# First norm of a transformer-like layer: gain and bias moved behind the transposes, and in token layout into the down stage

## The chip, the cores and the metric

One core of a Trainium2 chip runs the whole layer in one launch. The time is the device time of one execution in microseconds (us); the figure to compare is the median of several runs. Five engines work side by side: PE (matrix products), DVE (vector work), ACT (activations, copies and products with a scale), POOL (a slower vector engine) and SP, whose queue issues most of the transfers. Each works off its own instructions in the order in which the program was built, and stops where an instruction needs something that is not there yet.

## What is computed

One layer with 1024 tokens of width 1024: two mixing groups, an output projection, a residual and a layer norm, then a gated MLP of width 2816 with a causal convolution of width three on the gate branch, again a residual and a layer norm. The part that the change touches is the first norm and what reads its result:

```python
y = (xf - mu) * lax.rsqrt(var + LN_EPS) * g + b     # layer_norm
x = layer_norm(x * alpha + mix @ w_out, ln1_g, ln1_b)
h = causal_dwconv(x @ w_gate, conv_w, conv_b)
x = layer_norm(x * alpha + (silu(h) * (x @ w_up)) @ w_down, ln2_g, ln2_b)
```

So the normalised x is used twice: as the operand of the gate and up products, and as the residual behind the down product.

## The kernel before

Tokens lie in eight tiles t = 0 to 7 of 128 partitions. All large products are made in three matmuls each (`mm3`, L221 to L223) of 128x512, from operands that are split into a high part (ACT, L216) and a low part (DVE, L217).

**Output projection and first norm.** For each t PE makes the projection. `fill_x` adds the residual (DVE, L900) and takes the statistics (L901). `lnorm` then aggregates them (DVE, L882), adds epsilon (L884), raises to the power -1/2 (POOL, L885), and per half row subtracts the mean and multiplies by g (DVE, L887), scales (ACT, L889) and adds b (POOL, L890); for t = 7 DVE does the last step (L892). The rows g1 and b1, 128x1024 each, are loaded by POOL's queue (L873) ahead of that.

**Transposes.** `x1_transp(t)` transposes the eight 128x128 blocks of a tile (PE, L926), four to a PSUM bank, so that the width lies on partitions. ACT copies the blocks out (L934) and splits them; for A22 DVE adds A21 to the block straight out of PSUM (L931, the operand S1) and POOL forms A11 - A21 (L932). The tile's halves are called A11, A12 (tiles 0 to 3) and A21, A22 (tiles 4 to 7).

**Gate and up.** The stage uses Strassen-Winograd products: for each of 22 weight columns u seven products P1 to P7 of 12 matmuls each, instead of eight. Their left operands are A11, A12, A22 and the sums S1 = A21 + A22, S2 = S1 - A11, S3 = A11 - A21, S4 = A12 - S1. `x1_sums` makes S2 (DVE, L944) and S4 (POOL, L946) and splits all four; `w_prep` makes the sums of the weights (DVE, L968) and splits them. The first products need only A11 and A12, so tiles 6 and 7 and the sums are made between them (the list `fill_in`).

**Down stage.** The seven products run in the order P1, P2, P6, P5, P7, P4, P3, each over 11 steps m, from operands yo and do that `d_prepare` makes ahead; a pool of 20 slots holds them. Where a quarter of the output is done, DVE adds the residual x (L1223) and the second norm follows (`finish`). A pool of 16 larger slots (`kslot`) holds operands and rows.

The order on each engine is set where the program is built: it follows the order of the code and the slots that come free, not a table.

Of the kernel before, what the change touches and what calls it, by code (L numbers as in the profile page):

```python
# [138 lines left out]
def hybrid_layer_kernel(  # L139
# [90 lines left out]
    lam4 = const.tile([P, 4, 64], F32, name="lam4")  # L230
# [640 lines left out]
    def load_row(pool, ap_, name):  # L871
        t = pool.tile([P, D], F32, name=name)
        GP.dma_start(t, bc_row(ap_, D))  # L873
        return t

    g1 = load_row(op, ln1_g, "g1")
    b1 = load_row(op, ln1_b, "b1")
    x1T = {}
# [60 lines left out]
    def x1_sums(name):  # L939
        o = {"S1": "S1", "S2": "S1", "S3": "A21", "S4": "A12"}[name]  # L940
        x_operand(name, xslot if name in ("S1", "S2") else kslot)
# [314 lines left out]

    for n, name in enumerate(DORDER):
# [79 lines left out]
```

## Time and profile before

| | us |
|---|---|
| median of 3 runs | 1104.15 (1103.53 to 1104.35) |
| the profiled execution | 1102.54, its span 1100.8 |
| input projections | 0 to about 245 |
| attention | to about 375 |
| output projection, first norm, transposes | to about 455 |
| gate and up | 442 to 876 |
| down | 866 to 1092 |
| last norm and store | to 1100.8 |

The times of rows are counted from the span's start. A row of a timeline has the start, the length, the engine, the line, the operation, what it writes and reads, and how many instructions stand in it; a bracket at its end tells how long the engine was idle before it and what it waited for. Instructions that follow each other without a pause overlap a little, so the step from one to the next is shorter than the length shown: two of 1.21 in a row show 2.35 together.

### The profile page before, as it was taken

What the parts mean: (1) busy time and instruction counts of PE and PEld (TensorE: products, weight loads), DVE (VectorE), ACT (ScalarE), POOL (GpSimd) and SP (SyncE); (2) the same over time, 40 slices, a digit from 0 to 9 for tenths busy, and PEclk for the clock granted to TensorE, in tenths of its full rate; (3) what the DMA queues carried; (4) which work ended last, traced back from release to release, by engine and by line L of the source; (5) the groups of instructions that cost most, each with busy time, mean ns of one, the idle gap of its engine ahead of it and who ended that gap; (6) DMA issues with size and microseconds to landing.
All of it is one profiled execution on the core that took longest, in us unless ns stands there. A gap on an engine that the chain in (4) does not pass through costs nothing.

```text
span 1100.8 us, 13950 instructions
## 1 busy us (share of the span) xinstructions
PE 1063.5 (97%) x4974; PEld 873.8 (79%) x4974; DVE 806.4 (73%) x1331; ACT 488.1 (44%) x908; POOL 213.5 (19%) x233
## 2 busy tenths in 40 slices
PE   8999999889999999899999999999999999999995
PEld 6888887667788888678888888888888878888874
DVE  5327257789998648997787677778767679965786
ACT  5511113338777416564345344434534354444441
POOL 2014144466545126500000000000000000000045
PEclk9999999998999999999999999999999999999998
DMA  8400202111200421023323331332234883433322
GB/s 260 148 10 10 96 21 59 56 39 39 78 11 11 141 93 45 20 88 123 124 86 105 112 125 60 115 125 108 74 115 156 301 307 98 142 94 98 102 89 96
DMA packets 53222, 109.62 MB, mean 100 GB/s; under 512 B 6112, under 2 KB 6640, under 8 KB 53152
## 3 DMA queue, kind: packets, MB, share of 16 engines
q1 hardware_dynamic: 52112, 105.41, 28.4%
q0 software_dynamic: 1040, 3.32, 1.1%
q8 instruction: 39, 0.64, 0.3%
q14 instruction: 31, 0.25, 0.1%
HBM read 82.23 MB, written 24.38 MB: 97 GB/s over the span
## 4 chain that ended last, share of the span: by engine, by line
PE 78%; DVE 13%; POOL 2%; issue 2%; ACT 2%; DMA 1%; SPq 0%; DVEq 0%; POOLq 0%; ACTq 0%
PE ps L222 24%; PE ps L223 24%; PE ps L221 24%; DVE t L439 2%; PE ps L618 2%; POOL t L442 1%; DVE qs L471 1%; DVE p L587 1%; DVE x L887 1%; PE ps L604 1%; POOL uT L363 1%; PE ps L541 1%; DVE mx L554 1%; PE ps L542 1%; DMA xraw<-xT 1%
## 5 line engine op out<-in xcount | busy, mean ns | idle before, releaser
L222 PE MATMUL ps<-do,yo 128*128 128x512 f32 x308 | 120.9, 393 | 3.3 <-DVE do L217 3.3
L221 PE MATMUL ps<-do,yo 128*128 128x512 f32 x308 | 120.0, 391 | 2.5 <-ACT do L216 2.5
L223 PE MATMUL ps<-do,yo 128*128 128x512 f32 x308 | 120.3, 391 | 0.0
L1264 POOL DMA_DIRECT2D g<-ln_g x1 | 0.6, 578 | 476.0 <-DVE do L217 476.0
L217 DVE TENSOR_TENSOR wT<-wq,wT 128x512 fp32r<-128x512 f32 x88 | 63.1, 719 | 33.9 <-ACT wT L216 33.9
L216 ACT ACTIVATE wT<-wq 128x512 fp32r<-128x512 f32 x88 | 55.3, 632 | 50.2 <-PE ps L223 43.5
L217 DVE TENSOR_TENSOR yo<-ya,yo 128x512 fp32r<-128x512 f32 x77 | 55.0, 715 | 24.1 <-ACT yo L216 23.8
L222 PEld LDWEIGHTS ps<-do,yo 128*128 128x128 f32 x308 | 58.2, 189 | 16.8 <-DVE do L217 4.6
L221 PEld LDWEIGHTS ps<-do,yo 128*128 128x128 f32 x308 | 58.0, 189 | 15.2 <-ACT do L216 2.9
L216 ACT ACTIVATE yo<-ya 128x512 fp32r<-128x512 f32 x77 | 48.3, 627 | 48.1 <-PE ps L223 46.0
L223 PEld LDWEIGHTS ps<-do,yo 128*128 128x128 f32 x308 | 58.2, 189 | 11.9
L217 DVE TENSOR_TENSOR wB<-wq,wB 128x512 fp32r<-128x512 f32 x66 | 45.9, 698 | 27.0 <-ACT wB L216 20.6
L217 DVE TENSOR_TENSOR do<-dq,do 128x512 fp32r<-128x512 f32 x66 | 47.4, 718 | 22.4 <-ACT do L216 22.4
L968 DVE TENSOR_TENSOR wq<-wq,wq 128x512 f32<-128x512 f32 x88 | 60.7, 691 | 2.8 <-DMA wq<-w_up 0.2
L216 ACT ACTIVATE wB<-wq 128x512 fp32r<-128x512 f32 x66 | 41.1, 630 | 48.7 <-PE ps L223 33.5
L216 ACT ACTIVATE do<-dq 128x512 fp32r<-128x512 f32 x66 | 41.2, 624 | 46.6 <-DVE yo L217 17.4
L1034 DVE SCALAR_TENSOR_TENSOR c<-g,cw,c 128x1023 f32<-128x1023 f32 (+1 forms) x44 | 56.3, 1280 | 6.5 <-ACT c L1032 6.4
L223 PE MATMUL ps<-xh,qw 128*128 128x512 f32 x128 | 51.1, 400 | 4.2 <-DVE qw L217 4.2
L221 PE MATMUL ps<-xh,qw 128*128 128x512 f32 x128 | 50.7, 396 | 2.1 <-ACT qw L216 2.1
L566 ACT ACTIVATE p<-ps,mx 128x384 f32<-128x384 f32 (+7 forms) x64 | 47.4, 744 | 8.5 <-DVE mx L556 5.5
L222 PE MATMUL ps<-xl,qw 128*128 128x512 f32 x128 | 50.3, 393 | 0.0
L221 PE MATMUL ps<-zw,xh 128*128 128x512 f32 x128 | 49.8, 389 | 0.0
(243 smaller groups left out, 2986.6 us busy)
## 6 DMA issues: line engine op xcount, KB each, us to landing
ya<-yd SPq DMA_DIRECT2D x77, 256.0 KB, 3.0
wq<-w_gate SPq DMA_DIRECT2D x44, 256.0 KB, 2.8
wq<-w_up SPq DMA_DIRECT2D x44, 256.0 KB, 2.8
yd<-u SPq DMA_DIRECT2D x22, 512.0 KB, 3.1
dq<-w_down SPq DMA_DIRECT2D x44, 256.0 KB, 4.5
zraw<-w_vz SPq DMA_DIRECT2D x23, 256.0 KB, 3.1
yd<-c SPq DMA_DIRECT2D x11, 512.0 KB, 2.6
qraw<-w_qk SPq DMA_DIRECT2D x8, 512.0 KB, 3.7
```

The source lines that it names most:

```text
L216: A.activation(hi, src, AF.Copy)
L217: (lo_eng or V).tensor_tensor(lo, src, hi.bitcast(F32), op=ALU.subtract)
L221: PE.matmul(po, lhsT=lh, rhs=rh, start=start, stop=False, skip_group_check=onto)
L222: PE.matmul(po, lhsT=lh, rhs=rl, start=False, stop=False, skip_group_check=onto)
L223: PE.matmul(po, lhsT=ll, rhs=rh, start=False, stop=stop, skip_group_check=onto)
L363: GP.tensor_tensor(u, u, gt.rearrange("p c t -> p (c t)"), op=ALU.mult)
L439: eng.tensor_tensor(t[2][o], pt[i], sin_s[i, cols], op=ALU.mult)
L442: GP.tensor_tensor(t[1], t[1], t[2], op=ALU.add)
L566: A.activation(p[:, 0:L].rearrange("p (b n) -> p b n", b=nb), sc, AF.Exp, bias=st_mx[n][:, j : j + 1], accum_out=sm[:, j : j + 1],)
L618: PE.matmul(st_o[h, i][:, j * DV : (j + 1) * DV], lhsT=st_at[h, i][kt // 4][:, kt % 4, j], rhs=vr[kt // 2][:, kt % 2, h * DV : (h + 1) * D ...
L968: sub = lambda o, a, b: V.tensor_tensor(q[o], q[a], q[b], op=ALU.subtract)
L1034: V.scalar_tensor_tensor(t[:, n:S], g[:, 0 : S - n], cw[:, f, 2 - n : 3 - n], t[:, n:S], op0=ALU.mult, op1=ALU.add)
```

## The change

The first norm is taken apart. `standard(t)` only standardises: it makes -mean beside the standard deviation's power (POOL, power and a product of one column), and ACT applies both to the whole tile in one instruction of 1024 columns (L900). `x1_transp` takes two tiles at a time, two blocks of each to a bank, and ACT applies g and b while it evacuates (L938, 256 columns, scale and bias per partition, from the small tile `gb1`). S1 is now a sum of evacuated tiles on DVE (L943), and S3 and S4 are DVE's too (L953). The residual needs g and b as well: `gain` applies them in token layout in the down stage, 32 DVE instructions of 512 columns (L1269), with the rows g1 and b1 loaded there by POOL's queue (L1276). Last, `d_prepare` runs up to three steps further ahead in P4 and P3. The second norm keeps `lnorm`.

```diff
+    def standard(t):
+        mv = op.tile([P, 32], F32, tag="mv", name=nm("mv"), bufs=3)[:, 0:3]
+        rs = op.tile([P, 32], F32, tag="rs", name=nm("rs"), bufs=3)[:, 0:2]
+        V.bn_aggr(mv[:, 0:2], stats[t])
+        V.tensor_scalar(rs[:, 0:1], mv[:, 1:2], EPS, None, op0=ALU.add)
+        V.tensor_scalar(mv[:, 2:3], mv[:, 0:1], -1.0, None, op0=ALU.mult)
+        GP.tensor_tensor(rs[:, 0:1], rs[:, 0:1], mhalf[:, 0:1], op=ALU.pow)
+        GP.tensor_tensor(rs[:, 1:2], rs[:, 0:1], mv[:, 2:3], op=ALU.mult)
+        A.activation(x1[t], x1[t], AF.Identity, scale=rs[:, 0:1], bias=rs[:, 1:2])
...
     def x1_transp(t):
-        tk = slice((t % 4) * P, (t % 4 + 1) * P)
+        tk = slice((t % 4) * P, (t % 4 + 2) * P)
...
-            pt = ps1().rearrange("p (e q) -> p e q", e=4)
-            for e in range(4):
-                PE.transpose(pt[:, e, :], x1[t][:, (eg * 4 + e) * P : (eg * 4 + e + 1) * P], ident)
             for n in range(2):
-                src = pt[:, 2 * n : 2 * n + 2, :]
-                if name == "A22":
-                    f = xf["A21"][n][:, :, tk]
-                    V.tensor_tensor(xf["S1"][n][:, :, tk], f, src, op=ALU.add)
-                    GP.tensor_tensor(f, xf["A11"][n][:, :, tk], f, op=ALU.subtract)
-                else:
-                    A.copy(xf[name][n][:, :, tk], src)
+                pt = ps1().rearrange("p (e q) -> p e q", e=2)
+                f = xf["S1" if name == "A22" else name][n][:, :, tk]
+                for e in range(2):
+                    k = eg * 4 + n * 2 + e
+                    for i in range(2):
+                        PE.transpose(pt[:, e, i * P : (i + 1) * P], x1[t + i][:, k * P : (k + 1) * P], ident)
+                    A.activation(f[:, e], pt[:, e], AF.Identity, scale=gb1[:, 0, k : k + 1], bias=gb1[:, 1, k : k + 1])
                 if name != "A21":
                     hi, lo = xo[name][n]
-                    split(hi[:, :, tk], lo[:, :, tk], src)
+                    split(hi[:, :, tk], lo[:, :, tk], f)
+                if name == "A22":
+                    V.tensor_tensor(f, xf["A21"][n][:, :, tk], f, op=ALU.add)
...
         for n in range(2):
-            if name == "S2":
-                V.tensor_tensor(xf[o][n], xf["S1"][n], xf["A11"][n], op=ALU.subtract)
-            elif name == "S4":
-                GP.tensor_tensor(xf[o][n], xf["A12"][n], xf["S1"][n], op=ALU.subtract)
+            if a:
+                V.tensor_tensor(xf[o][n], xf[a][n], xf[b][n], op=ALU.subtract)
             split(*xo[name][n], xf[o][n])
...
-        lnorm(op, x1[t], stats[t], x1[t], g1, b1, None, t < NT - 1)
-        if 2 <= t < 6:
-            x1_transp(t - 2)
+        standard(t)
+        if t in (3, 5):
+            x1_transp(t - 3)
...
-    fill_in = [
-        lambda: x1_transp(6), lambda: x1_transp(7), lambda: (x1_sums("S1"), prepare(1)),
-        lambda: (x1_sums("S2"), prepare(4), x1_sums("S3"), prepare(5), x1_sums("S4")),
-    ]
+    fill_in = {
+        2: lambda: x1_transp(6),
+        3: lambda: (x1_sums("S1"), prepare(1)),
+        4: lambda: (x1_sums("S2"), prepare(4), x1_sums("S3"), prepare(5), x1_sums("S4")),
+    }
...
+    def gain(t, c):
+        r = x1[t][:, RIGHT if c else LEFT]
+        for row, op_ in (("g1", ALU.mult), ("b1", ALU.add)):
+            V.tensor_tensor(r, r, rows[row][:, RIGHT if c else LEFT], op=op_)
+    gains = {("P1", 2 * j + 2): (j, 0) for j in range(4)}
+    gains.update({("P2", 2 * j + 1): (j, 1) for j in range(4)})
+    gains.update({("P5", j + 1): (4 + j % 4, 1 - j // 4) for j in range(8)})
...
-            d_prepare(n * NM + m + DAHEAD)
+            d_prepare(n * NM + m + DAHEAD + (max(0, min(3, m - 3)) if name == "P4" else 3 if name == "P3" else 0))
+            if (name, m) in gains:
+                gain(*gains[name, m])
```

What this does to the order is seen at three places. In the rows below x is a token tile, ps a PSUM bank, fA an evacuated tile in transposed layout, gb the small tile with g and b, A22h the high part of operand A22, wT, wB and wq weights; the numbers tell buffers apart.

ACT before, where tiles 4 and 5 are evacuated: the scaling of tile 6 (tile 7 has its on DVE), the copies, then splits and the first output of the gate stage.

```order
L889 ACTIVATE x_3614<-x_3614,rs_4060 128x512 x2
L934 COPY fA_4107<-ps_755_4115 128x2x128
L934 COPY fA_4108<-ps_755_4115 128x2x128
L934 COPY fA_4107<-ps_757_4135 128x2x128
L934 COPY fA_4108<-ps_757_4135 128x2x128
L216 ACTIVATE A22h_4109<-ps_756_4122 128x2x128
L216 ACTIVATE A22h_4109<-ps_758_4142 128x2x128
L1005 COPY g_4174<-ps_759_4161 128x512
```

ACT after, at the same place.

```order
L938 ACTIVATE fA_4068<-ps_755_4076,gb_83 128x256
L938 ACTIVATE fA_4069<-ps_756_4083,gb_83 128x256
L938 ACTIVATE fA_4074<-ps_757_4090,gb_83 128x256
L938 ACTIVATE fA_4068<-ps_755_4076,gb_83 128x256
L900 ACTIVATE x_3654<-x_3654,rs_4061 128x1024
L938 ACTIVATE fA_4069<-ps_756_4083,gb_83 128x256
L938 ACTIVATE fA_4074<-ps_757_4090,gb_83 128x256
L938 ACTIVATE fA_4075<-ps_758_4100,gb_83 128x256
L217 ACTIVATE A22h_4070<-fA_4074 128x2x256
```

The standardising of tile 7 (L900) now stands between the evacuations of tiles 4 and 5; PE's second pair of transposes into bank 758 waits for the third evacuation behind it.

ACT before, where S1h (the high part of S1) is made, from the last two splits of A22 on.

```order
L216 ACTIVATE A22h_4110<-ps_763_4184 128x2x128
L216 ACTIVATE A22h_4109<-ps_769_4226 128x2x128
L216 ACTIVATE S1h_4258<-fA_4113 128x1024
L1005 COPY u_4255<-ps_771_4242 128x512
L216 ACTIVATE A22h_4110<-ps_769_4226 128x2x128
L216 ACTIVATE S1h_4259<-fA_4114 128x1024
L216 ACTIVATE wT_4268<-wq_4199 128x512
L216 ACTIVATE wT_4300<-wq_4019 128x512
```

ACT after, at the same place.

```order
L938 ACTIVATE fA_4075<-ps_771_4194,gb_83 128x256
L217 ACTIVATE A22h_4070<-fA_4074 128x2x256
L938 ACTIVATE fA_4075<-ps_771_4194,gb_83 128x256
L217 ACTIVATE wT_4209<-wq_4134 128x512
L217 ACTIVATE A22h_4071<-fA_4075 128x2x256
L217 ACTIVATE wT_4239<-wq_3984 128x512
L217 ACTIVATE S1h_4225<-fA_4074 128x1024
L217 ACTIVATE S1h_4226<-fA_4075 128x1024
```

S1h stood ahead of the splits of the weights; now it stands behind the last evacuation, the splits of A22 and two of weights.

DVE before, at the end of the gate stage: the last output yd of the convolution (L1046), then the low part of operand do for step m = 4 of P1.

```order
L1044 TENSOR_TENSOR u_7129<-u_7129,c_7204 128x512
L1014 TENSOR_TENSOR u_7130<-u_7130,ps_1151_7236 128x512
L1020 TENSOR_TENSOR c_7228<-c_7228,u_7130 128x512
L1046 TENSOR_TENSOR u_7130<-c_7228,u_7129 128x512
L217 TENSOR_TENSOR do_7370<-dq_7340,do_7370 128x512
```

DVE after, at the same place (the last output is L1053 there).

```order
L1051 TENSOR_TENSOR u_7080<-u_7080,c_7155 128x512
L1027 TENSOR_TENSOR c_7179<-c_7179,u_7081 128x512
L1269 TENSOR_TENSOR x_3511<-x_3511,b_7286 128x512
L1053 TENSOR_TENSOR u_7081<-c_7179,u_7080 128x512
L1269 TENSOR_TENSOR x_3497<-x_3497,g_7284 128x512
L1269 TENSOR_TENSOR x_3486<-x_3486,g_7284 128x512
L1269 TENSOR_TENSOR x_3497<-x_3497,b_7286 128x512
```

From the last row on 15 of these instructions of `gain` follow each other up to the split of do for m = 4; 12 more stand between the steps of the convolution ahead of L1053.

## Rows read from the trace of the kernel before

**Rows 1.** The page's part 1: busy us, share, instructions of each engine.

```profile
PE 1063.5 (97%) x4974; PEld 873.8 (79%) x4974; DVE 806.4 (73%) x1331; ACT 488.1 (44%) x908; POOL 213.5 (19%) x233
```

**Rows 2.** Timeline of PE: projection, transposes of tiles 4 and 5, S1.

```profile
439.71 0.39 PE L221 MATMUL ps<-ow,oT 128*128 128x512 f32 x1
...
440.85 0.39 PE L223 MATMUL ps<-ow,oT 128*128 128x512 f32 x1
441.08 1.91 PE L926 MATMUL ps<-ident,x 128*128 128x128 f32 x16
442.74 0.48 PE L221 MATMUL ps<-A11h,wB 128*128 128x512 f32 x1
...
455.51 0.39 PE L221 MATMUL ps<-S1h,wT 128*128 128x512 f32 x1
```

**Rows 3.** Stretches: length; busy of PE, PEld, DVE, ACT, POOL; PE clock, DMA share, GB/s.

```profile
455.00:480.00 25.00, 18.56 (x65) 13.18 (x65) 25.00 (x26) 13.27 (x19) 6.31 (x3) 0.86 0.16 52
465.00:470.00 5.00, 4.61 (x11) 3.12 (x11) 5.00 (x4) 0.00 (x0) 1.28 (x1) 0.50 0.00 0
1070.00:1085.00 15.00, 11.66 (x43) 8.55 (x42) 11.65 (x17) 2.67 (x4) 8.87 (x7) 0.89 0.19 71
```

**Rows 4.** Timelines of DVE and PE at the change to the down stage.

```profile
855.52 0.68 DVE L1007 TENSOR_TENSOR u<-u,ps 128x512 f32<-128x512 f32 x1
...
859.82 1.28 DVE L1034 SCALAR_TENSOR_TENSOR c<-g,cw,c 128x1023 f32<-128x1023 f32 x1 [2.42 <-ACT c L1032]
...
873.54 0.69 DVE L1020 TENSOR_TENSOR c<-c,ps 128x512 f32<-128x512 f32 x1 [1.70 <-PE ps L223]
...
887.79 0.69 DVE L217 TENSOR_TENSOR do<-dq,do 128x512 fp32r<-128x512 f32 x1 [9.39 <-ACT do L216]
...
887.81 1.21 PE L221 MATMUL ps<-do,yo 128*128 128x512 f32 x4 [2.52 <-ACT do L216]
```

**Rows 5.** Waits of PE, 365 to 458: us in total, times, longest.

```profile
PE ps L222 <- DVE S1l L217: 0.5, 1, 0.5
```

**Rows 6.** Timelines of DVE, POOL and ACT, norm of tiles 6 and 7 and S1 to S4.

```profile
435.83 0.69 DVE L900 SCALAR_TENSOR_TENSOR x<-xn,ps 128x512 f32<-128x512 f32 x1 [1.54 <-PE ps L223]
...
441.28 0.69 DVE L900 SCALAR_TENSOR_TENSOR x<-xn,ps 128x512 f32<-128x512 f32 x1 [1.28 <-PE ps L223]
...
454.59 1.76 DVE L217 TENSOR_TENSOR S1l<-fA,S1h 128x1024 fp32r<-128x1024 f32 x1
...
458.93 2.35 DVE L944 TENSOR_TENSOR fA<-fA,fA 128x1024 f32<-128x1024 f32 x2
461.20 2.84 DVE L217 TENSOR_TENSOR wT<-wq,wT 128x512 fp32r<-128x512 f32 x1
463.97 4.52 DVE L217 TENSOR_TENSOR S2l<-fA,S2h 128x1024 fp32r<-128x1024 f32 x2
...
477.18 1.89 DVE L217 TENSOR_TENSOR wT<-wq,wT 128x512 fp32r<-128x512 f32 x3
...
437.83 0.99 POOL L885 TENSOR_TENSOR rs<-rs,mhalf 128x1 f32<-128x1 f32 x1 [1.15 <-DVE rs L884]
...
460.23 6.05 POOL L946 TENSOR_TENSOR fA<-fA,fA 128x1024 f32<-128x1024 f32 x2 [4.97 <-DVE fA L944]
...
455.75 1.15 ACT L216 ACTIVATE wT<-wq 128x512 fp32r<-128x512 f32 x2
```

**Rows 7.** Groups by line and shape: busy us, mean ns of one, idle before.

```profile
L1032 ACT ACTIVATE c<-g,cb,cw 128x1024 f32<-128x1024 f32 x22 | 27.3, 1242 | 10.7 <-DVE g L1014 10.7
...
L664 ACT ACTIVATE oT<-ps,sg 128x256 fp32r<-128x256 f32 x16 | 7.6, 475 | 7.8 <-PE ps L658 7.7
...
L216 ACT ACTIVATE S1h<-fA 128x1024 fp32r<-128x1024 f32 x2 | 2.1, 1062 | 0.0
...
L652 POOL TENSOR_TENSOR o<-o,rs 128x256 f32<-128x256 f32 x8 | 5.8, 730 | 0.5
```

**Rows 8.** Transfers: queue, count, KB each, median us from issue to landing.

```profile
g<-ln_g POOLq DMA_DIRECT2D x2, 512.0 KB, 5.1
```

More of the change, by code (lines that the diff above doesn't have):

```diff
@@ L163, in hybrid_layer_kernel @@
     sin_t: bass.AP,
+    ln1_c: bass.AP,
     out: bass.AP,
@@ L229, in hybrid_layer_kernel @@
     m_r = const.tile([P, 64], BF16, name="m_r")
-    lam4 = const.tile([P, 4, 64], F32, name="lam4")
+    const.tile([P, 42], F32, name="pad")
     nlam = const.tile([P, 1], F32, name="nlam")
@@ L234, in hybrid_layer_kernel @@
     cb = const.tile([P, NF], F32, name="cb")
+    gb1 = const.tile([P, 2, NK], F32, name="gb1")
     zp = tc.alloc_tile_pool(name="zp", bufs=1)
@@ L285, in hybrid_layer_kernel @@
     glb = zq.tile([P, ATT], F32, name="glb")
+    lam4 = zp.tile([P, 4, 64], F32, name="lam4")
     wsr = zp.tile([P, H, P], F32, name="wsr")
@@ L295, in hybrid_layer_kernel @@
     GP.dma_start(cb, conv_b)
+    GP.dma_start(gb1, ln1_c)
     GP.affine_select(
@@ L869, in hybrid_layer_kernel @@
     op = tc.alloc_tile_pool(name="op", bufs=1, reuse_waits="tile")
[L871 to L878, printed above, removed]
     def lnorm(pool, r, st, o, g, b, after=None, spread=False):
-        mv = pool.tile([P, 32], F32, tag="mv", name=nm("mv"), bufs=3)[:, 0:2]
+        mv = pool.tile([P, 2], F32, tag="mv", name=nm("mv"), bufs=3)
         V.bn_aggr(mv, st)
-        rs = pool.tile([P, 32], F32, tag="rs", name=nm("rs"), bufs=3)[:, 0:1]
+        rs = pool.tile([P, 1], F32, tag="rs", name=nm("rs"), bufs=3)
         V.tensor_scalar(rs, mv[:, 1:2], EPS, None, op0=ALU.add)
@@ L923, in x1_transp @@
         for eg, name in enumerate(names):
[L924 to L926 removed]
             for n in range(2):
[L928 to L934 removed]
+                pt = ps1().rearrange("p (e q) -> p e q", e=2)
[5 more added lines that the diff above has]
+                    A.activation(f[:, e], pt[:, e], AF.Identity, scale=gb1[:, 0, k : k + 1], bias=gb1[:, 1, k : k + 1])
                 if name != "A21":
                     hi, lo = xo[name][n]
[L937 removed]
+                    split(hi[:, :, tk], lo[:, :, tk], f)
+                if name == "A22":
+                    V.tensor_tensor(f, xf["A21"][n][:, :, tk], f, op=ALU.add)
     def x1_sums(name):
+        a, b, slot = {
+            "S1": (None, None, xslot), "S2": ("S1", "A11", xslot), "S3": ("A11", "A21", kslot), "S4": ("A12", "S1", kslot)
+        }[name]
         o = {"S1": "S1", "S2": "S1", "S3": "A21", "S4": "A12"}[name]
[L941 removed]
+        x_operand(name, slot)
         for n in range(2):
[L943 to L946 removed]
+            if a:
+                V.tensor_tensor(xf[o][n], xf[a][n], xf[b][n], op=ALU.subtract)
             split(*xo[name][n], xf[o][n])
@@ L1092, in hybrid_layer_kernel @@
     x1_transp(4)
-    x1_transp(5)
-    fp = None
     NU = NF
@@ L1187, in hybrid_layer_kernel @@
     dram = tc.alloc_tile_pool(name="dram", bufs=1, space=bass.MemoryType.DRAM)
-    fill_in = [
-        lambda: x1_transp(6), lambda: x1_transp(7), lambda: (x1_sums("S1"), prepare(1)),
-        lambda: (x1_sums("S2"), prepare(4), x1_sums("S3"), prepare(5), x1_sums("S4")),
-    ]
+    fill_in = {
[3 more added lines that the diff above has]
+    }
     for i, (u, name) in enumerate(seq):
         prepare(max(0, i + AHEAD - 4))
+        if i == 4:
+            fill_in[i]()
         product(u, name)
+        if i < 4 and i in fill_in:
+            fill_in[i]()
         outputs(u, name)
-        if i < len(fill_in):
-            fill_in[i]()
         if (u, name) == (NU - 1, "P2"):
@@ L1255, in finish @@
         lnorm(wdp[0], r, stats2[t], r, rows["g2"], rows["b2"], store, spread)
+    def gain(t, c):
[5 more added lines that the diff above has]
+    gains.update({("P5", j + 1): (4 + j % 4, 1 - j // 4) for j in range(8)})
+    for r, src in (("g1", ln1_g), ("b1", ln1_b)):
+        rows[r] = kslot([P, D], r, F32)
+        GP.dma_start(rows[r], bc_row(src, D))
     for n, name in enumerate(DORDER):
@@ L1328 @@
         "sin_t": lay(np.concatenate([sin, -sin] * 2, axis=0)),
+        "ln1_c": lay(np.stack([v["ln1_g"][0].reshape(NK, P).T, v["ln1_b"][0].reshape(NK, P).T], axis=1)),
     }
```

## The prediction

> **What bounds the kernel now.** I read the page's busy times first: PE is busy 97% of the span [rows 1], so time can only be won where PE stands still, and anything that makes it stand still costs its full length. Undisturbed matmuls follow each other every 0.228 us (439.71 to 440.85 are five steps [rows 2]). Then the stretches, to find where fewer fit in. In 455 to 480 there are 65 [rows 3]: 65 x 0.228 = 14.8, so 10.2 of 25 us are lost. In 1070 to 1085 there are 43: 9.8 of 15, 5.2 us lost. A third hole, 2.5 us, ends at 887.81 [rows 4]. From 365 to 458, through the out-projection and the norm, the list of waits has a single one of PE, 0.5 us [rows 5]: work that the change takes off DVE and POOL there buys no time.
>
> The timeline of the first hole shows why it is there. DVE is busy for all of 455 to 480 [rows 3] with the operands S1 to S4. Two POOL instructions of 3.0 us each, L946, start at 460.23, and the DVE rows beside them stretch: a split of 512 columns takes 2.84 us (alone 0.60, the third part of the row at 477.18), the two of S2l take 4.52 (1.135 each, the step of the pair at 458.93) [rows 6]. That is (2.84 - 0.68) + (4.52 - 2.35) = 4.3 us of DVE time, on the chain that PE waits for; the S1l at 454.59 lost another 0.5 beside L932. Granted clock falls to half in 465 to 470 [rows 3].
>
> **Part one, the norm and the transposes.** POOL is left with a power and a one-column product per token tile; that removes the stretching, worth up to 4.8 us on DVE, but not for nothing. The transposes now go in pairs of tiles: eight, then three times two with a single matmul between. The second pair in a PSUM bank waits until ACT has evacuated the first. In the order, three times ACT has the standardising L900 of the tile just finished in front of evacuations that PE needs. At the last such place: call T the moment when PE begins transposing tiles 4 and 5. DVE begins with tile 7 at T + 0.20 (441.28 against 441.08); from there to the end of the power it is 437.83 + 0.99 - 435.83 = 3.0 [rows 2, 6]. The one-column product is not in the trace: between next to nothing and 0.73 (a 256-column product, L652 [rows 7]); I take 0.25, as most of that is its columns. L900 has 1024 columns with scale and bias per partition, as L1032, 1.24 (low: 1.06, a plain split of that width) [rows 7]. The evacuation L938 is nearest to L664, 0.475 with one per-partition operand; the second adds (1.24 - 1.06) / 2 = 0.09, so 0.57, a step of 0.46 in a row.
>
> The Trainium skill (ScalarE: Activation LUTs, section What ACT_TABLE_LOAD costs) has 186 ns plus 0.833 ns an element and some 93 ns for each per-partition operand; that would be 0.585 for L938 as an estimate. L664 [rows 7] with its single operand agrees with it (0.49); no row here has the operation itself. By the page the sum below is 0.05 larger, by L664 alone 0.4 smaller.
>
> ACT therefore ends the third evacuation behind L900 at T + 0.2 + 3.0 + 0.3 + 1.14 + 2 x 0.46 + 0.57 = T + 6.1. PE reaches the transpose behind it after 14 transposes of 0.104 (16 in 1.66), 14 matmuls and four changes from transposes to matmuls at 0.09 (the first matmul behind them shows 0.48, the others 0.39) [rows 2]: T + 5.0. It waits 1.1. The same sum gives 1.0 at the first pair (L900 of tile 3, three evacuations and two splits of 0.52 ahead, against 14 transposes and 19 matmuls) and 0.9 at the second (L900 of tile 4, late because DVE makes four splits between its steps). Small waits at the other banks, 0.6 in all, and nine more changes between transposes and matmuls at 0.09, 0.8: **+4.3 us** together. With the low prices 2.0, with the high ones 5.8. Nothing hides it, since PE had no idle time there.
>
> **Part two, operands S1 to S4.** Before, DVE made S1 straight out of PSUM, piece by piece, so S1h could start at once. Now the sum needs the evacuated A22 of all four tiles. Take as zero PE's arrival at the first S1 matmul (455.51 before [rows 2]). ACT's queue from the last pair of transposes is one evacuation, three splits of 512 (0.52 each, from the pair at 455.75) and S1h (1.06): PE starts at +2.8, where it started at 0 before. S1l then takes 1.2 and PE waits 1.1 again. From there DVE has 14 instructions of 1024 columns (four more than before, the sums of S3 and S4 that POOL made) and nine of 512: 14 x 1.135 + 9 x 0.60 = 21.3 us. The same stretch took 454.59 to 478.98 = 24.4 before [rows 6]: shorter by 3, but begun 3 to 4 later. PE's further waits by this walk: 1.0 for S2l, 2.5 for the S3 split of ACT that stands behind the second S3 sum, 1.9 for DVE's half of it, 2.0 for the weights of T2 and 0.2 behind. Sum 11.5, against 10.2 lost before: **+1.3 us**. Low: -1, if one of the two late waits falls under the other; high: +3.5, if the clock falls as in 465 to 470, where 11 matmuls took 5 us.
>
> **Part three, g and b in the down stage.** 32 instructions of 512 columns at 0.60 are 19 us on DVE. Five stand in P5, where DVE has room. 27 stand between 857 and the operand of m = 4. The first two stand ahead of the convolution and wait for the row g1, whose slot comes free with the matmuls that DVE's row at 855.52 waits for, about 855.2; with issue and 5.1 us to landing [rows 8] that is 860.9, and the convolution, which began at 859.82 [rows 4], begins at 862.1. Up to the sum that began at 873.54, DVE now has 17 steps of 0.60 and four of 1.19: 860.9 + 15.0 = 875.9, late by 2.4; three more gains and latencies, and the last product yd ends at 881.6 instead of 878.4 (887.79 - 9.39). The 15 gains behind it take 9.1: DVE comes to the split of m = 4 at 890.7 and ends it at 891.4, where it ended at 888.5 (887.79 and 0.69). Its load, issued behind the stores of yd, is late by up to 3 us too, and has two loads fewer ahead. PE's hole of 2.5 us grows by **+2.7 us** (0.8 if the row lands early enough for the pauses of DVE to take the gains; 4 if the load is late by all of the 3.2 and transfers share). The rows on POOL's queue and two slots fewer cost nothing elsewhere: the operands of P2 and P6 stand far enough ahead.
>
> **Part four, preparing ahead.** The built orders of DVE and ACT from the end of P4 on are those of before: the 20 operand slots decide, and the last splits stay behind the final norms. So the 5.2 us of 1070 to 1085 stay: **0** (low: -5.2, were they to move). The small row for g and b at the start lies beside the first loads: 0.
>
> **Sum:** 4.3 + 1.3 + 2.7 = +8.3 us. The profiled execution took 1102.54 (span 1100.8), so it would become 1110.8; it was 1.6 below the median of the runs shown, 1104.15, and against that the forecast is 1112.4.
>
> **Rivals.** *POOL's hold is the whole loss (faster).* If S1 begins no later than before relative to PE's arrival, because ACT clears the last evacuations quicker than the walk says, DVE's 24.4 us become about 18 to 20 and the first hole shrinks by the 4.8 of stretching. With the low ends of parts one and three (2.0 and 0.8) that is -2 to -3: 1101.3. For it: DVE is full there, and the stretched rows are plain. Against: three splits and an evacuation stand ahead of S1h in ACT's queue. It decides at a wait for S1h under 0.5 us. 12%. *Everything at its low end (no change):* 2.0 - 1 + 0.8 = +1.8: 1105.9. 13%. *The preparing ahead works after all:* 8.3 - 5.2 = +3.1: 1107.3. The order speaks against it. 5%. *The clock falls in the longer wait for S1h* and S1's 24 matmuls run at half speed, as after the waits at 460 to 465: 24 x 0.2 = 4.8, half of it beside DVE's work: 1115 to 1117. 10%. The forecast itself has 60%.
>
> **How the numbers follow.** A measurement of this kernel can tell about 0.2% (2.2 us) from no change. Faster is the first rival, 12%; within 0.2% the second, 13%; all others are slower, 75%. The range leaves out the first rival and the upper end of the clock case, and takes in the low ends of all three parts: 1104 to 1118.
>
> **What would show it.** Right: PE waits of about 1 us each on ACT's L938 at three places before 455; a first S1 matmul that waits 2 to 3 us for S1h; DVE splits beside no POOL work at 0.6 and 1.14; a hole before m = 4 of 5 us instead of 2.5, with DVE busy with L1269 up to it; 1070 to 1085 as before. Wrong: no waits at the transposes, or S2l ready when PE comes to it. Most exposed is part one: the price of the one-column product and of L938 is in no row.

## The result

The changed kernel is slower: 1116.68 us median of four runs (1113.63 to 1117.34) against 1103.84 for the kernel before in the same comparison (four runs, 1102.67 to 1104.35). The ratio is 1.0106, with a 95% interval of 1.0087 to 1.0125, so some 9.6 to 13.8 us; the medians differ by 12.8. The forecast was 1112.4, the range 1104 to 1118. The profiled execution of the changed kernel took 1116.12, its span 1114.4; 13.6 more than the span before.

### Where the 13.6 us lie

PE runs the same 4974 instructions in both kernels, so points of the program can be set side by side. Four serve here: the first matmul of the output projection that reads oT, PE's arrival at the first S1 matmul (its start less its wait), the first matmul of the down stage, and the last one. The rows of PE's timeline, first of the kernel before (its S1 row is in [rows 2]):

```profile
359.10 0.48 PE L221 MATMUL ps<-ow,oT 128*128 128x512 f32 x1
...
865.89 0.39 PE L221 MATMUL ps<-do,yo 128*128 128x512 f32 x1
...
1091.99 0.39 PE L223 MATMUL ps<-do,yo 128*128 128x512 f32 x1
```

And of the changed kernel (lines of `mm3` are one further on, L222 to L224; the high and low splits are L217 and L218):

```profile
360.38 0.48 PE L222 MATMUL ps<-ow,oT 128*128 128x512 f32 x1
...
463.27 1.22 PE L222 MATMUL ps<-S1h,wT 128*128 128x512 f32 x2 [2.69 <-ACT S1h L217]
...
872.35 0.39 PE L222 MATMUL ps<-do,yo 128*128 128x512 f32 x1
...
1105.56 0.39 PE L224 MATMUL ps<-do,yo 128*128 128x512 f32 x1
```

| stretch | before | changed | difference | predicted |
|---|---|---|---|---|
| start to first oT matmul | 359.10 | 360.38 | +1.28 | 0 |
| to PE's arrival at S1 | 96.41 | 100.20 | +3.79 | +4.3 |
| to the first down matmul | 410.38 | 411.77 | +1.39 | +1.3 |
| to the last matmul | 226.10 | 233.21 | +7.11 | +2.7 |
| to the end | 8.81 | 8.84 | 0 | 0 |

The first 1.28 us lie ahead of everything that the change touches; in the eleven traces of this study that point lies anywhere between 358.94 and 362.85. So the time of one execution carries a scatter of up to 3.9 us that has nothing to do with an edit, and the stretches are the finer measure. The norm and the sums cost almost what was predicted, the change to the down stage nearly three times as much.

### The rows that answer to those of before

The page's part 1, to set against [rows 1]: PE's busy time is longer by 5.7 us although its work is the same. Of these, 3.2 us are matmuls behind new waits that ran at half clock, as the rows below show.

```profile
PE 1069.2 (96%) x4974; PEld 875.5 (79%) x4974; DVE 812.8 (73%) x1341; ACT 495.1 (44%) x898; POOL 180.9 (16%) x218
```

The list of PE's waits (us in total, times, longest), 362 to 520, where [rows 5] had a single one up to 458:

```profile
PE ps L222 <- ACT wT L217: 3.9, 2, 2.1
PE ps L222 <- ACT S1h L217: 2.7, 1, 2.7
PE ps L937 <- ACT fA L938: 1.9, 3, 0.7
PE ps L224 <- DVE wT L218: 0.6, 1, 0.6
PE ps L223 <- DVE S1l L218: 0.5, 1, 0.5
```

The three waits for the evacuation L938 are the transposes behind the standardising. Behind S1 the list has 7.7 us; the kernel before has 6.5 there (2.3, 1.7, 1.6, 0.5 and 0.4, for weights, S2 and S1). The difference is 1.2 of the 1.39 in the third line of the table.

The same list from 850 on. The kernel before has 2.5 for do of m = 4 [rows 4] and the same 3.3 in P3.

```profile
PE ps L222 <- ACT do L217: 4.2, 1, 4.2
PE ps L223 <- DVE do L218: 3.3, 3, 1.3
PE ps L222 <- ACT u L1016: 2.3, 1, 2.3
```

The last of these is new and stood in no step of the prediction. Its story is in three timelines, DVE's, ACT's and PE's:

```profile
868.35 1.29 DVE L1269 TENSOR_TENSOR x<-x,g 128x512 f32<-128x512 f32 x2 [4.48 <-DMA g<-ln_g]
869.56 1.28 DVE L1041 SCALAR_TENSOR_TENSOR c<-g,cw,c 128x1023 f32<-128x1023 f32 x1
870.75 0.68 DVE L1021 TENSOR_TENSOR g<-g,ps 128x512 f32<-128x512 f32 x1
...
871.47 1.25 ACT L1039 ACTIVATE c<-g,cb,cw 128x1024 f32<-128x1024 f32 x1 [5.21 <-DVE g L1021]
...
875.13 0.56 ACT L1016 COPY u<-ps 128x512 f32<-128x512 f32 x1
...
875.74 0.59 PE L222 MATMUL ps<-S3h,wT 128*128 128x512 f32 x1 [2.32 <-ACT u L1016]
876.13 0.63 PE L223 MATMUL ps<-S3l,wT 128*128 128x512 f32 x1
```

DVE stands 4.48 us in front of the first gain, because the row g1 has not landed. The gate's convolution is behind it. ACT's convolution step at 871.47 waits for a sum of DVE (L1021), and the copy L1016 is behind that step. L1016 empties the PSUM bank that PE needs for S3. So one late transfer goes through three engines in order. Matmuls behind this wait show 0.63 and steps of 0.43 instead of 0.39 and 0.23: from 875.74 nine of them take 3.75 us instead of 2.05. The stretch of 875 to 880 has a granted clock of 0.66 (length; busy of PE, PEld, DVE, ACT, POOL; PE clock, DMA share, GB/s):

```profile
875.00:880.00 5.00, 4.26 (x12) 3.36 (x13) 5.00 (x9) 1.75 (x3) 0.00 (x0) 0.66 0.64 193
```

Then m = 4, in the order ACT, DVE, PE:

```profile
899.28 0.63 ACT L217 ACTIVATE do<-dq 128x512 fp32r<-128x512 f32 x1 [18.31 <-DMA dq<-w_down]
899.94 0.69 DVE L218 TENSOR_TENSOR do<-dq,do 128x512 fp32r<-128x512 f32 x1 [1.03 <-ACT do L217]
899.96 2.07 PE L222 MATMUL ps<-do,yo 128*128 128x512 f32 x4 [4.15 <-ACT do L217]
```

DVE is idle for 1.03 ahead of its split: the gains were over, and ACT waited for the load dq. The 15 gains behind the last output L1053 had ended at 898.9. PE's wait is 4.15 instead of 2.52, and the four matmuls behind it show 2.07 instead of 1.21 [rows 4]; with the next four it is 3.49 instead of 1.98. The 7.11 us are therefore 2.32 + 1.70 (the wait for L1016 and the half clock behind it) + 1.63 + 1.51 (the longer wait before m = 4 and the half clock behind that) = 7.16.

Why the load came late is seen in DVE's rows, of the kernel before and then of the changed one:

```profile
876.26 0.69 DVE L1014 TENSOR_TENSOR u<-u,ps 128x512 f32<-128x512 f32 x1
```

```profile
886.78 0.69 DVE L1021 TENSOR_TENSOR u<-u,ps 128x512 f32<-128x512 f32 x1 [0.23 <-PE ps L224]
...
888.60 0.68 DVE L1269 TENSOR_TENSOR x<-x,b 128x512 f32<-128x512 f32 x1
889.20 0.68 DVE L1053 TENSOR_TENSOR u<-c,u 128x512 f32<-128x512 f32 x1
```

L1021 sums PE's last S4 product, and PE is late by then. The down stage as a whole begins 6.46 us later in the changed kernel (872.35 against 865.89); beyond that L1021 is 4.06 late, about what PE lost at S3 (2.32 + 1.70). The last yd ends at 889.88 instead of 878.40, 0.96 later still: one gain and L1051 stand between. From there to ACT's half of the operand it is 9.40 instead of 8.73, 0.67 more. Together the operand is 5.69 late, and PE's wait grows by the 1.63 that it had not lost before.

### The profile page after: what moved, and what is told of

It reads as the page before. It is cut to its first block, busy times and chain, and to the rows that moved or that the text cites. A ratio compares the mean times of both kernels' runs of the same rounds, so it can differ in the third digit from the quotient of the medians.

```text
span 1114.4 us, 13895 instructions
## 1 busy us (share of the span) xinstructions
PE 1069.2 (96%) x4974; PEld 875.5 (79%) x4974; DVE 812.8 (73%) x1341; ACT 495.1 (44%) x898; POOL 180.9 (16%) x218
## 4 chain that ended last, share of the span: by engine, by line
PE 61%; DVE 13%; issue 5%; ACT 3%; POOL 2%; DMA 1%; SPq 0%; DVEq 0%; POOLq 0%; ACTq 0%
PE ps L222 19%; PE ps L223 19%; PE ps L224 19%; PE ps L622 2%; DVE t L443 2%; POOL t L446 1%; DVE p L591 1%; DVE x L882 1%; PE ps L608 1%; PE ps L545 1%; DVE qs L475 1%; DVE mx L558 1%; PE ps L546 1%; DVE fA L953 1%; DVE qw L218 1%
## 5 line engine op out<-in xcount | busy, mean ns | idle before, releaser
L222 PE MATMUL ps<-do,yo 128*128 128x512 f32 x308 | 120.9, 394 | 4.2 <-ACT do L217 4.2
L224 PE MATMUL ps<-do,yo 128*128 128x512 f32 x308 | 120.7, 392 | 0.0
L218 DVE TENSOR_TENSOR wT<-wq,wT 128x512 fp32r<-128x512 f32 x88 | 60.4, 688 | 34.2 <-ACT wT L217 34.2
L217 ACT ACTIVATE wT<-wq 128x512 fp32r<-128x512 f32 x88 | 55.5, 632 | 48.6 <-PE ps L224 43.9
L222 PEld LDWEIGHTS ps<-do,yo 128*128 128x128 f32 x308 | 58.5, 190 | 16.7 <-ACT do L217 4.6
L217 ACT ACTIVATE yo<-ya 128x512 fp32r<-128x512 f32 x77 | 48.3, 627 | 51.6 <-PE ps L224 48.8
L218 DVE TENSOR_TENSOR yo<-ya,yo 128x512 fp32r<-128x512 f32 x77 | 54.9, 713 | 21.2 <-ACT yo L217 21.0
L224 PEld LDWEIGHTS ps<-do,yo 128*128 128x128 f32 x308 | 58.5, 190 | 12.2
L1276 POOL DMA_DIRECT2D g<-ln_g x1 | 0.6, 632 | 414.3 <-PE ps L224 414.3
L218 DVE TENSOR_TENSOR wB<-wq,wB 128x512 fp32r<-128x512 f32 x66 | 45.4, 689 | 26.7 <-ACT wB L217 26.3
L217 ACT ACTIVATE wB<-wq 128x512 fp32r<-128x512 f32 x66 | 41.4, 630 | 50.2 <-PE ps L224 35.3
L217 ACT ACTIVATE do<-dq 128x512 fp32r<-128x512 f32 x66 | 41.1, 623 | 45.8 <-DMA dq<-w_down 18.3
L218 DVE TENSOR_TENSOR do<-dq,do 128x512 fp32r<-128x512 f32 x66 | 47.3, 717 | 14.2 <-ACT do L217 13.9
L224 PE MATMUL ps<-xh,qw 128*128 128x512 f32 x128 | 51.0, 399 | 3.8 <-DVE qw L218 3.8
L222 PE MATMUL ps<-xh,qw 128*128 128x512 f32 x128 | 50.7, 396 | 1.6 <-ACT qw L217 1.6
L222 PE MATMUL ps<-zw,xh 128*128 128x512 f32 x128 | 49.8, 389 | 0.0
```

Source lines behind the costliest of these rows:

```text
L217: A.activation(hi, src, AF.Copy)
L218: (lo_eng or V).tensor_tensor(lo, src, hi.bitcast(F32), op=ALU.subtract)
L222: PE.matmul(po, lhsT=lh, rhs=rh, start=start, stop=False, skip_group_check=onto)
L224: PE.matmul(po, lhsT=ll, rhs=rh, start=False, stop=stop, skip_group_check=onto)
```

## The experiments

The theory after this reading: the loss has three places. The evacuations and S1h wait in ACT's queue behind the standardising; the late row g1 holds DVE, ACT and PE; the loads for m = 4 come late behind the late last outputs. The rival for the last two is the prediction's own step, that DVE's time for the gains ahead of m = 4 decides. Each kernel ran beside the kernel before, whose median was 1105.16 beside e1 to e4 (16 runs, 1102.63 to 1107.72), 1105.27 beside e5 to e8 (22 runs, 1102.46 to 1107.93) and 1105.14 beside e9. Line numbers move by a few from kernel to kernel.

### e1: without the gains

```diff
-    for r, src in (("g1", ln1_g), ("b1", ln1_b)):
-        rows[r] = kslot([P, D], r, F32)
-        GP.dma_start(rows[r], bc_row(src, D))
...
-            if (name, m) in gains:
-                gain(*gains[name, m])
```

> The changed kernel without the 32 gains and without the two rows g1 and b1 in the down stage; the residual of the down product therefore lacks g and b. The stretch up to 865 stays as in the changed kernel. Theory (the gains and their row cost about 7 us at the change to the down stage, the norm and the sums the other 7): about 1109.5 us, no wait of PE for the gate copy at 875, the wait before m = 4 back to 2.5 us. Rival (the loss sits in the norm and the sums, and the waits seen at the change of stage only take the place of others): within 2 us of the changed kernel, 1115 to 1117.

Measured: 1110.23 us (1109.25 to 1112.05), ratio 1.0049 (1.0031 to 1.0067). From the first down matmul to the last 225.95 (873.74 to 1099.69), where the changed kernel has 233.21 and the kernel before 226.10. The wait for the gate copy is gone, the one before m = 4 is back at 2.4:

```profile
PE ps L223 <- DVE do L218: 3.3, 3, 1.3
PE ps L222 <- ACT do L217: 2.4, 1, 2.4
```

The 7.1 us of the down stage belong to the gains and their rows, and nothing of them only moved. What is left, 5.15 us from the first oT matmul to the first down matmul, is the norm and the sums.

### e2: the gains behind the operand of m = 4

```diff
-    gains = {("P1", 2 * j + 2): (j, 0) for j in range(4)}
+    gains = {("P1", j + 6): (j, 0) for j in range(4)}
...
-    for r, src in (("g1", ln1_g), ("b1", ln1_b)):
...
+            if (name, m) == ("P1", 3):
+                for r, src in (("g1", ln1_g), ("b1", ln1_b)):
+                    rows[r] = kslot([P, D], r, F32)
+                    GP.tensor_copy(rows[r][:, 0:1], dop["P1", 4][1][:, 1, 0:1].bitcast(F32))
+                    GP.dma_start(rows[r], bc_row(src, D))
```

The copy of one column makes the load wait for that operand; the load then overwrites it.

> All 32 gains stay, but the rows are loaded only when the operand of m = 4 is split, so that every gain stands behind it, in P1, P2 and P5. Theory (not the DVE time of the gains costs, but their place ahead of the last column's outputs): within 1 us of the kernel without gains, about 1110. Rival (19 us more on DVE cost wherever they stand): about 1115, with new waits of PE for operands in P1, P2 or P5.

Measured: 1107.19 us (1106.34 to 1110.22, ten runs), ratio 1.0025 (1.0013 to 1.0038). All 32 gains are there, 685 ns each, and no wait of PE comes from them:

```profile
PE ps L223 <- DVE do L218: 3.3, 3, 1.3
```

The rival falls: 19 us of DVE cost nothing behind m = 4. But the theory's number was missed too, on the good side. First to last down matmul took 223.36 (875.54 to 1098.90), 2.7 less than before the change: the wait before m = 4, which the kernel before had already, is gone. The order on SP's queue offers a reason. The rows take two large slots, so loads of weights for later m, which stood ahead of the last stores of yd and of the load for m = 4, now stand behind them. e6 tests that by itself.

### e3: the gains wait for the last yd, not the row

```diff
+        if (u, name) == (NU - 1, "P3"):
+            for r, src in (("g1", ln1_g), ("b1", ln1_b)):
+                rows[r] = kslot([P, D], r, F32)
+                GP.dma_start(rows[r], bc_row(src, D))
+                GP.tensor_copy(rows[r].rearrange("p (c n) -> p c n", c=2)[:, :, 0:1], dst_w[u][1].rearrange("p (c n) -> p c n", c=2)[:, :, 0:1])
...
-    for r, src in (("g1", ln1_g), ("b1", ln1_b)):
-        rows[r] = kslot([P, D], r, F32)
-        GP.dma_start(rows[r], bc_row(src, D))
```

> The rows are loaded as early as in the changed kernel, but the first gain may start only when the last product yd is ready; 14 gains still stand between it and the operand of m = 4 (the first column of each half of the rows is overwritten to force this). It tells the late landing of row g1, which holds DVE, ACT and PE, from the DVE time ahead of m = 4. Theory (the landing): the 2.3 us wait for the gate copy and the half clock behind it are gone and yd is stored on time; 1110 to 1111. Rival (the 14 gains hold the operand of m = 4, as the prediction had it): the wait before m = 4 stays at 4 us or more and only the 2.3 + 1.6 us go: about 1113.

Measured: 1110.55 us (1108.87 to 1113.01), ratio 1.0052 (1.0032 to 1.0072). First to last down matmul 227.34 (873.53 to 1100.87): 5.9 of the 7.1 us are gone, although 14 gains stand between the last yd and do of m = 4. The rows of DVE, then ACT:

```profile
885.28 0.69 DVE L1053 TENSOR_TENSOR u<-c,u 128x512 f32<-128x512 f32 x1
886.26 1.29 DVE L1274 TENSOR_TENSOR x<-x,g 128x512 f32<-128x512 f32 x2 [0.29 <-POOL g L1212]
...
893.50 1.29 DVE L1274 TENSOR_TENSOR x<-x,g 128x512 f32<-128x512 f32 x2
895.01 0.69 DVE L218 TENSOR_TENSOR do<-dq,do 128x512 fp32r<-128x512 f32 x1 [0.22 <-ACT do L217]
...
894.35 0.63 ACT L217 ACTIVATE do<-dq 128x512 fp32r<-128x512 f32 x1 [16.34 <-DMA dq<-w_down]
```

The gains end at 894.8, and ACT, which waited for the load alone, ends its half at 895.0. So the gains fill the time that the load takes anyway, and PE waits 2.2 (2.52 before the change). That the stretch is still 1.24 longer is half clock behind that wait: the first ten matmuls took 3.98 us instead of 2.44. So the gains behind the last yd cost PE nothing, and the prediction's step for this place falls. The twelve gains ahead of the last yd are gone in e3 as well, so e3 alone does not separate them from the landing of g1. The timeline of the changed kernel does: the 4.48 us in which DVE waits for g1 lead to PE's wait before S3; behind that, one gain stands on the chain to m = 4, 0.6 us.

### e4: DVE standardises

```diff
-        GP.tensor_tensor(rs[:, 1:2], rs[:, 0:1], mv[:, 2:3], op=ALU.mult)
-        A.activation(x1[t], x1[t], AF.Identity, scale=rs[:, 0:1], bias=rs[:, 1:2])
+        V.tensor_scalar(x1[t], x1[t], mv[:, 0:1], rs[:, 0:1], op0=ALU.subtract, op1=ALU.mult)
```

> The standardising of a tile is made by DVE in one instruction of 1024 columns instead of by ACT; the product -mean times rs on POOL falls away. The down stage stays as in the changed kernel. Theory (the evacuations wait behind the standardising in ACT's queue): the three waits of PE for evacuations, 1.9 us together, fall under 0.6, and the first S1 matmul comes 1.5 to 2.5 us earlier, about 1115 in all. Rival (the waits come from the number of evacuations alone, or from the transposes in pairs): the three waits stay within 0.4 us, 1116 to 1117.

Measured: 1111.97 us (1111.35 to 1115.58), ratio 1.0058 (1.0039 to 1.0077). The waits for evacuations are gone from the list altogether:

```profile
PE ps L222 <- ACT S1h L217: 2.9, 1, 2.9
PE ps L222 <- DVE g L1017: 2.6, 1, 2.6
PE ps L223 <- DVE S1l L218: 1.1, 1, 1.1
PE ps L222 <- ACT g L1014: 0.7, 1, 0.7
```

PE arrives at S1 97.55 us after the first oT matmul, 2.65 earlier than with ACT's standardising (100.20), and 1.14 later than before the change. So about 2.7 of the norm's 3.8 us are the standardising in ACT's queue with what feeds it; with no wait left, 1.1 remain; that these are the transposes in pairs with single matmuls between them is argued, not shown. The wait for S1h did not shrink: ACT's queue ahead of it is the last evacuation and the splits, not the standardising. DVE's instruction of 1024 columns took 0.81 us, ACT's 1.25. The down stage, unchanged, again cost 8 us more than before.

### e5: both edits

The edits of e2 and e4 together:

```diff
+        V.tensor_scalar(x1[t], x1[t], mv[:, 0:1], rs[:, 0:1], op0=ALU.subtract, op1=ALU.mult)
...
+                    GP.tensor_copy(rows[r][:, 0:1], dop["P1", 4][1][:, 1, 0:1].bitcast(F32))
```

> Standardising by DVE and the gains behind the operand of m = 4, both edits of the two runs before in one kernel. Theory (the two losses lie in different stretches and add up): from the first output-projection matmul to the first down matmul 509.5 us, as with DVE's standardising alone, from there to the last matmul 223.4 us, as with the late gains alone; about 1104.5. Rival (each edit's gain was partly the same slack): above 1106.5.

Measured: 1103.36 us (1101.56 to 1105.94, ten runs), ratio 0.9979 (0.9964 to 0.9993). First oT to first down matmul 508.26, from there to the last 223.67. The gains add, and the sum is a little faster than the kernel before. But the down stage is shorter by 2.4 through the order on SP's queue, which is no part of the change, as e6 shows; the stretch of the norm and the sums is still 1.5 longer than before.

### e6: the kernel before, with the loads in another order

```diff
             d_prepare(n * NM + m + DAHEAD)
+            if (name, m) == ("P1", 3):
+                hold = [kslot([P, D], "hold", F32) for _ in range(2)]
+                for t_ in hold:
+                    GP.tensor_copy(t_[:, 0:1], dop["P1", 4][1][:, 1, 0:1].bitcast(F32))
```

> The kernel before, with one thing added: two of the large slots are held until the operand of m = 4 is split, by two copies of one column on POOL. This puts the stores of the last yd and the loads for m = 4 ahead of some ten loads for later m on SP's queue, as the late gains did by accident. Theory (PE's 2.5 us before m = 4 come from the order on SP's queue, not from DVE): that wait goes, no new one comes, from the first down matmul to the last 223.4 instead of 226.1 us, about 2.7 us faster than the kernel before. Rival (the ten loads are needed soon after): new waits of PE for operands in P1 or P2, no gain.

Measured: 1101.14 us (1099.44 to 1103.08, nine runs), ratio 0.9966 (0.9955 to 0.9978); first to last down matmul 223.31. ACT's row for m = 4, before and then here:

```profile
887.13 0.63 ACT L216 ACTIVATE do<-dq 128x512 fp32r<-128x512 f32 x1 [16.73 <-DMA dq<-w_down]
```

```profile
883.82 0.63 ACT L216 ACTIVATE do<-dq 128x512 fp32r<-128x512 f32 x1 [12.66 <-DMA dq<-w_down]
```

SP's queue around the last store of yd, before and then here (the last column is the number of transfers issued):

```profile
866.08 9.39 SPq L1154 DMA_DIRECT2D dq<-w_down  x12
...
878.43 0.32 SPq L1050 DMA_DIRECT2D yd<-u  x1
878.80 5.07 SPq L1154 DMA_DIRECT2D dq<-w_down  x7
```

```profile
866.87 0.86 SPq L1154 DMA_DIRECT2D dq<-w_down  x2
...
879.15 0.32 SPq L1050 DMA_DIRECT2D yd<-u  x1
879.56 2.63 SPq L1154 DMA_DIRECT2D dq<-w_down  x4
```

Twelve loads stood ahead of the last three stores and two do here; in the built order three more stood between the last store and the load for m = 4, which here follows the store directly. The last yd ends at 878.40 before and at 879.12 here. From there to the operand it was 8.7 us and is 4.7. In the stretch of 875 to 880 the DMA engines are busy for 0.99 before and for 0.41 here. No wait came in exchange: PE's list from 850 on has the 3.3 us of P3 alone, so the loads were not needed soon.

### e7: the kernel before, S4 on DVE

```diff
-                GP.tensor_tensor(xf[o][n], xf["A12"][n], xf["S1"][n], op=ALU.subtract)
+                V.tensor_tensor(xf[o][n], xf["A12"][n], xf["S1"][n], op=ALU.subtract)
```

> The kernel before, with the two sums of S4 made by DVE instead of POOL; nothing else. Theory (POOL's two instructions of 3.0 us each hold DVE, 4.3 us in all, and two sums of 1.2 on DVE cost less): the splits beside them show 0.60 and 1.14, PE's waits between 458 and 480 fall by 1.5 to 2.5 us, about 2 us faster than the kernel before. Rival (the waits there belong to ACT's queue and to the order): within 0.7 us of the kernel before.

Measured: 1101.30 us (1099.36 to 1103.10, eight runs), ratio 0.9962 (0.9949 to 0.9975). First oT to first down matmul 504.69 against 506.79: 2.1 us less. DVE's timeline where [rows 6] had 2.84 and 4.52:

```profile
462.11 0.68 DVE L217 TENSOR_TENSOR wT<-wq,wT 128x512 fp32r<-128x512 f32 x1
462.71 2.35 DVE L217 TENSOR_TENSOR S2l<-fA,S2h 128x1024 fp32r<-128x1024 f32 x2
...
467.86 2.35 DVE L946 TENSOR_TENSOR fA<-fA,fA 128x1024 f32<-128x1024 f32 x2
```

So the reading of POOL's hold was right: 4.3 us of stretching go and two sums of 1.2 come, which leaves about 2. On PE the waits behind S1 fall from 6.5 to 5.1, by 1.4, a little less than expected. The rest is the clock: granted 0.50 in 465 to 470 before, 1.00 in 466 to 471 here and 0.69 in the 5 us after that. e6, which is the kernel before up to the down stage, took 507.74 for this stretch, and e9 504.68, so the gain is 2 to 3 us. The rows agree with the Trainium skill (SBUF — State Buffer, section SBUF: two separate sides), by which DVE's operations with two SBUF inputs and POOL's that read SBUF take a shared port pair from each other for a whole instruction. In the changed kernel the splits of S2l take 2.35 too (at 470.05), but they lie behind the later start of S1.

### e8: without the further preparing ahead

```diff
-            d_prepare(n * NM + m + DAHEAD + (max(0, min(3, m - 3)) if name == "P4" else 3 if name == "P3" else 0))
+            d_prepare(n * NM + m + DAHEAD)
```

> The changed kernel without the further preparing ahead in P4 and P3. Theory (that edit changes nothing, since slots decide): the three waits for do in P3 stay 0.7, 1.3 and 1.3 us, within 1 us of the changed kernel. Rival (it gives something that the other losses hide): slower than the changed kernel by 2 us or more.

Measured: 1115.10 us (1113.96 to 1116.78), ratio 1.0086 (1.0062 to 1.0110), an interval that overlaps that of the changed kernel (1.0087 to 1.0125). PE's waits in P3 are 3.3 us in three, the longest 1.3, in this kernel, in the changed one and in e1 to e4. The edit does nothing that these runs can tell.

### e9: the kernel before with e6 and e7

```diff
+                V.tensor_tensor(xf[o][n], xf["A12"][n], xf["S1"][n], op=ALU.subtract)
...
+                hold = [kslot([P, D], "hold", F32) for _ in range(2)]
```

> The kernel before with both edits of the two runs above, the held slots and the S4 sums on DVE. The two waits lie in different stages (before m = 4, and 458 to 480), so theory: the gains add, from the first output-projection matmul to the first down matmul 504.7 us, from there to the last 223.3 us, about 1097 to 1098. Rival (the time won in the first stage comes back as a wait for the last column's transfers): 1100 or more.

Measured: 1099.63 us (1098.20 to 1101.32, five runs) beside 1105.14 of the kernel before (nine runs), ratio 0.9944 (0.9931 to 0.9958). This is the fastest kernel of the study. The stretches are those expected, 504.68 and 223.25 us; 5.0 less than before together. The median missed its number, 1097 to 1098. The profiled execution took 1101.32, with the first oT matmul at 362.52 instead of 359 to 360, in a part of the program that no edit touched; it was the slowest of the five, so this does not show why the median missed.

| kernel | to first oT | oT to down | down to last | median |
|---|---|---|---|---|
| before | 359.10 | 506.79 | 226.10 | 1105.2 |
| changed | 360.38 | 511.97 | 233.21 | 1116.7 |
| e1 | 361.80 | 511.94 | 225.95 | 1110.2 |
| e2 | 362.85 | 512.69 | 223.36 | 1107.2 |
| e3 | 360.67 | 512.86 | 227.34 | 1110.6 |
| e4 | 361.24 | 509.50 | 234.31 | 1112.0 |
| e5 | 360.49 | 508.26 | 223.67 | 1103.4 |
| e6 | 358.94 | 507.74 | 223.31 | 1101.1 |
| e7 | 359.97 | 504.69 | 226.09 | 1101.3 |
| e8 | 360.37 | 514.00 | 231.87 | 1115.1 |
| e9 | 362.52 | 504.68 | 223.25 | 1099.6 |

The stretches are of one execution each: that of before took 1102.54, 2.7 below the median shown, and that of e4 1115.58, 3.6 above its own. The changed kernel's median stood beside 1103.84 of the kernel before.

Between kernels that are alike up to the down stage (changed, e1, e2, e3, e8) the column oT to down differs by up to 2.1. Their waits there add up to 7.7 to 8.4; PE's arrival at S1 is the same within 0.06. What remains is the half clock among the S products, which differs from trace to trace: in 485 to 490 the granted clock was 0.72 in e8 and 1.00 in the changed kernel.

## Why the prediction was right or wrong

**What bounds the kernel.** Right. PE's work is the same, and but for the transposes and some of the first S products so is its order. The differences are waits of PE, the clock behind them, and the 1.1 us that e4 leaves ahead of S1 without a wait.

**Part one, +4.3; measured +3.8.** Right in its mechanism: three waits for L938 at the three places named, and e4 removes them together with the standardising in ACT's queue. The waits were 0.56, 0.70 and 0.61 instead of 1.0, 0.9 and 1.1, so 1.87 in place of 3.0. What else there is came to 1.92 in place of 1.4; the total is closer than its terms. (As written the terms add up to 4.4, and with L664's price three evacuations make 0.3 less, not 0.4.) The term that was too large is POOL's. The groups by line of the changed kernel, 410 to 470 (busy us, mean ns):

```profile
L898 POOL TENSOR_TENSOR rs<-rs,mhalf 128x1 f32<-128x1 f32 x6 | 3.6, 605 | 33.3 <-DVE mv L897 33.3
L899 POOL TENSOR_TENSOR rs<-rs,mv 128x1 f32<-128x1 f32 x6 | 1.2, 192 | 0.5
L938 ACT ACTIVATE fA<-ps,gb 128x256 f32<-128x256 f32 x32 | 15.9, 564 | 3.3 <-PE ps L937 3.2
L900 ACT ACTIVATE x<-x,rs 128x1024 f32<-128x1024 f32 x7 | 8.7, 1245 | 16.1 <-POOL rs L899 16.1
```

The power took 0.605 where it took 0.99 before the change [rows 6], and the product 0.19 where 0.25 was assumed: 0.45 less ahead of L900, which is what the first and the last wait lack (0.44 and 0.49; the second lacks 0.20). L938 and L900 came as priced from [rows 7], 0.57 and 1.24. By the Trainium skill (ScalarE: Activation LUTs, section What ACT_TABLE_LOAD costs) L938 was estimated at 0.585; the measured 0.564 lies between that and L664's 0.475, and nearer to the first.

**Part two, +1.3; measured +1.4.** Right in its first step: PE waited 2.69 for S1h (predicted 2.8). That the total agrees is luck. The walk behind had 1.1 for S1l, 1.0 for S2l, 2.5 and 1.9 for S3 and 2.0 for weights; measured were 0.55 for S1l, none for S2l, 2.15 and 0.61 before S3 (for weights, not for S3's split) and 1.71 for the next weights: 7.7 in all instead of 11.5. Most of the rest is half clock, which the sum left out: the 13 matmuls from 463.27 to 469.87 took 3.1 us more than at 0.228 each, at a granted clock of 0.52 in 465 to 470.

Nor is +1.4 sharp. From PE's arrival at S1 to the first down matmul the five kernels that are alike there took 411.70 to 413.80, the kernel before and e6 410.38 and 411.29: a difference anywhere between 0.4 and 3.4. The rival that POOL's hold was the whole loss had to have a wait for S1h under 0.5: it falls. The hold itself was real (e7).

**Part three, +2.7; measured +7.1. The step that failed.** The prediction had the row's late landing, and moved the convolution to 862.1 for it. In the terms of the kernel before it began at 863.1 (869.56 less the 6.46 by which the down stage is later): the transfer took 6.4 us and not the 5.1 of [rows 8]:

```profile
g<-ln_g POOLq DMA_DIRECT2D x1, 512.0 KB, 6.4
```

But the mistake is what came after. The prediction followed DVE's lateness only through DVE, down to the operand of m = 4, and took the 15 gains there for the late one, the load only for the upper end. ACT, which stands in order behind DVE's sum, and PE, which needs a bank that ACT empties, were not followed; that alone is 2.32 us of waiting and 1.70 of half clock, and it makes PE's last S4 product and with it the last yd late. At m = 4 the load decided, not the gains behind the last yd (e3): the operand was 5.69 late instead of 2.7. The half clock behind the longer wait, 1.5 us, was left out as well. The forecast of 1112.4 fell short by 4.3 us, and this term by 4.4. The measured terms, 3.8 + 1.4 + 7.1 = 12.3, add up to the 12.8 between the medians but for half a microsecond.

**Part four, 0; measured 0.** Right: the three waits in P3 stay, with the further preparing ahead and without it (e8), and the rival that it works after all falls.

**The rival on the clock** had 1115 to 1117, and the median is 1116.68, but not by its mechanism. It was placed at S1 and priced there with 24 matmuls. The clock did fall there, for 13 of them, as it fell in 465 to 470 before the change [rows 3]; the half clock that came on top of the forecast's part three, 3.2 us, was in the down stage.

## What to carry to other kernels

When work that waits for a transfer is put into an engine's queue, follow the wait through every engine that stands in order behind it, up to the PSUM bank that PE needs; here 4.5 us on DVE became 4.0 on PE by way of ACT. Allow for half clock behind each new wait of PE, 1.5 to 1.7 us at the two places here, and do not price it with its length alone; behind some waits of this length no half clock came. And where a wait ends with a load, look at what stands ahead of that load on its queue: some ten transfers that nobody needed soon cost the kernel before 2.8 us (226.10 against 223.31).

## What the runs showed of the hardware

- POOL's power of one column took 0.99 us in the kernel before and 0.605 in the changed kernel, 0.545 in e4, with the same operands. No run tells why; in the kernel before POOL also adds b between the powers.
- DVE's `tensor_scalar` of 1024 columns with two operands per partition took 0.81 us, where two-tensor operations of that width take 1.2 (L946 in e7).
- Behind waits of PE of 2.2 to 4.2 us the granted clock fell to half for eight to ten matmuls in some traces. Behind the 2.5 us of the kernel before [rows 4] and the 2.4 of e1 it did not, behind the 2.2 us of e3 at the same place it did; no run tells why.
